# Border to the up projection: the third f pair's raw weights loaded from ScalarE's queue, and split behind the second pair's first chain

## The chip, the cores and the metric

The kernel runs on one core of one Trainium2 chip. The metric is the device time of one execution in microseconds (us), as the median of several runs. The names of the engines are those of the profile: PE is TensorE (PEld its weight loads), DVE VectorE, ACT ScalarE, POOL GpSimd, SP SyncE. SPq and ACTq are the instruction queues of SP and ACT, from which DMAs are issued.

## The reference

One inference step of a hybrid encoder layer, for 1024 prompt frames and 64 sample frames. The part that matters here is the second sub-layer, an MLP with a squared ReLU, and its first matrix product:

```python
def sq_relu_mlp(x, w_up, w_down):
    h = jnp.square(jax.nn.relu(jnp.einsum('btd,df->btf', x, w_up)))
    return jnp.einsum('btf,fd->btd', h, w_down)
...
xp = layer_norm(ALPHA * xp + mix, ln1_g[l], ln1_b[l])
xp = layer_norm(ALPHA * xp + sq_relu_mlp(xp, w_up[l], w_down[l]), ln2_g[l], ln2_b[l])
```

Here `x` has 1024 columns and `w_up` is 1024 x 4096. The layer norm ahead of it closes the mixer; the product with `w_down` follows.

## The kernel before

All matrix products run in three passes of split fp32: each operand is a high part (rounded to the PE's fp32r form by an ACT copy, line 1247 or 1531) and a low part (the difference, line 98, on POOL or DVE). The up projection goes over 16 pairs of 128 columns of `w_up` (`p`, an "f pair"), and in each pair over two groups of columns of x, `s` = 0 (288 wide, the sample frames among them) and `s` = 1 (256 wide). Each (pair, group) is one *chain* of seven products in place of eight (a Strassen-like scheme), of twelve matmuls each, at line 1309. A product needs one of seven weight operands: 0, 1 and 3 are raw quarters of the pair's weights (tile `wa`), 2, 4, 5 and 6 are sums of quarters (tile `ws`).

The seven products of a chain add into four PSUM banks named zA, zB, zC and zD:

```python
PROD = ((0, 0, "A"), (1, 1, "B"), (5, 4, "A"), (4, 3, "D"), (6, 5, "A"), (3, 6, "C"), (2, 2, "D"))
```

So products 0, 2 and 4 add into the same bank zA, and between them ACT copies the bank out (line 1320): product 2 waits for ACT's copy of product 0, product 4 for that of product 2. Products 3 and 6 share zD: product 6 waits for DVE's sum at line 1323, which reads zD and the copy of product 4. DVE also makes the sums at 1325 (zB), 1327 (zC) and 1329 (zD after product 6). `relu` (line 1341) squares, `sums` (lines 1350 to 1353) makes the h operands of the down projection, and SP stores them (`h4_dr` at line 1354, `h3_dr` at 1355, `hs_dr` at 1358).

The weights of a pair are prepared by `prep`: the raw 1 MB is loaded into tile `wr` (line 1500 before, 1501 after the change), three quarters are split into `wa` (high halves by ACT at 1247; low halves at 98 by POOL, for pair 2 the first of them by DVE), `summed` forms the sums in place in `wr` by four DVE operations (1256, 1257, 1259, 1260), `high` and `low` split these into `ws` (1531 by ACT, 98 by DVE).

The stretch around the change is the *border* between the mixer and the steady loop over the pairs. There the order of each engine's instructions is written out by hand (`with in_order(border)`: each instruction is chained behind the one before it on its engine). First the two chains of pair 0 run, then the weights of pair 1 are prepared, then its chains `ch` (s = 0) and `ch1` (s = 1), and beside them the weights of pair 2 are prepared. From pair 2 on, the order of PE is kept by hand for pair 2 and otherwise found by a planner, which puts instructions in the order in which it expects them to be ready.

The framework adds the semaphores. Each DMA reports on one of eight semaphores (DMAHW0 to DMAHW7), taken in turn; the queue that issues a DMA first waits until the DMA that used the same semaphore before has landed. In the border the two stores of h of chain (0, 1), from the tiles `y`, take semaphores 4 and 5; those of chain (0, 0), from `h`, take 6, 7, 0, 1 and 2; the two halves of pair 2's raw load take 3 and 4.

Of the kernel before, what the change touches and what calls it, by code (L numbers as in the profile page):

```python
# [49 lines left out]
def build(tc, a):  # L50
    nc = tc.nc
    es = ExitStack()
    with es:
        _build(nc, tc, a, es)


def _build(nc, tc, a, es):
    def trows(t):
        return P if t < NB else TS
# [9 lines left out]
    w_up = a["w_up"].rearrange("l d e -> (l d) e").rearrange("(k p) e -> p k e", p=P)  # L69
# [30 lines left out]
    @contextmanager  # L100
    def in_order(prev=None, only=None):

        traced = nc.cur_bb.bb.instructions
        last = traced[-1]
        yield
        at = next(k for k in reversed(range(len(traced))) if traced[k] is last) + 1
        prev = {} if prev is None else prev
        for i in traced[at:]:
            if only is not None and i.engine != only:
                continue  # L110
            p = prev.get(i.engine)
            if p is not None:
                tc.add_manual_dep(i, p.name, mybir.DependencyInfo(
                    mybir.DependencyClass.NoSync, mybir.DependencyReason.DATA), reason="in_order")
            prev[i.engine] = i
# [53 lines left out]
    def two_halves(nm, sa, tag):  # L169
        if sa is not None:  # L170
            return [sa.tile([P, 512], F32, name=f"{nm}_{i}", tag=tag, bufs=10) for i in range(2)]
        r = sp.tile([P, D], F32, name=nm, tag="row", bufs=ROWS)
        return [r[:, 0:512], r[:, 512:D]]

    def prep(t, sa):
        n = trows(t)
        o = two_halves(f"oo{t}", sa, "kp")
        if sa is not None:
            uu = sa.tile([P, 256], F32, name=f"uu{t}", tag="uu", bufs=2)
            sqs = [sa.tile([P, 512], F32, name=f"sq{t}", tag="sq", bufs=1)] * 2  # L180
        else:
            uu = sp.tile([P, 256], F32, name=f"uu{t}", tag="gl", bufs=3)
            sqs = [sp.tile([P, 512], F32, name=f"sq{t}_{i}", tag="raw", bufs=2) for i in range(2)]
        nc.sync.dma_start(uu[0:n], u_dr[t * P:t * P + n, :])
        ss = sp.tile([P, 16], F32, name=f"ss{t}", tag="ss", bufs=2)
        for i in range(2):
            oh = o[i][0:n]
            nc.sync.dma_start(oh, o_dr[t * P:t * P + n, i * 512:(i + 1) * 512])
            c = slice(384, 512) if i == 0 else slice(0, 128)
            nc.gpsimd.tensor_tensor(oh[:, c], oh[:, c], uu[0:n, i * P:(i + 1) * P], op=ALU.mult)  # L190
            sq = sqs[i]
            nc.scalar.activation(sq[0:n], oh, AF.Square)
            sh = ss[0:n, i * 8:(i + 1) * 8]
            nc.vector.tensor_reduce(sh, sq[0:n].rearrange("p (h c) -> p h c", c=DH), axis=AX.X, op=ALU.add)
            nc.vector.scalar_tensor_tensor(sh, sh, 1.0 / DH, env["rge"][0:n, t, i * 8:(i + 1) * 8],
                                           op0=ALU.mult, op1=ALU.add)
            nc.gpsimd.tensor_tensor(sh, sh, negh[0:n].broadcast_to([n, 8]), op=ALU.pow)
            o3 = oh.rearrange("p (h c) -> p h c", c=DH)
            nc.vector.tensor_tensor(o3, o3, sh.unsqueeze(2).broadcast_to([n, 8, DH]), op=ALU.mult)
        os_[t] = o  # L200
# [89 lines left out]
    with ExitStack() as p1:  # L290
# [818 lines left out]
        while f_live or a_live:  # L1109
# [11 lines left out]
            if go_a:  # L1121
# [5 lines left out]
                try:  # L1127
                    c = next(A)
# [8 lines left out]
            elif f_live:  # L1137
                try:
                    c = next(F)
# [355 lines left out]
    with p3:  # L1495
        def up_load(p):
            r = lp.tile([P, KT, 256], F32, name=f"wr{p}", tag="wr")

            for c in ((0, P), (P, 256)) if p == 2 else ((0, 256),):
                nc.sync.dma_start(r[:, :, c[0]:c[1]], w_up[:, :, p * 256 + c[0]:p * 256 + c[1]])  # L1500
            return r[:, :, 0:P], r[:, :, P:256], r

        def prep(p, rest=True, raw=None):
            raw = raw or up_load(p)
            pool = rp if p % 2 else lp
            wa = pool.tile([P, 3, 2, 4, P], F32R, name=f"wa{p}", tag="wa")
# [39 lines left out]
        def chain(p, s):  # L1546
            sn = lp.tile([P, 2 + s, NS[s]], F32, name=f"sn{p}_{s}", tag=f"sn{s}")
            h8 = lp.tile([P, 8, NS[s]], F32, name=f"hh{p}_{s}", tag=f"hh{s}")
            return Chain(p, s, sn, lambda a, b: h8[:, a:b], ((2, 6),))
# [4 lines left out]
        with in_order(border):  # L1554
# [27 lines left out]
            summed, high, low = prep(1, False, raws1)  # L1582
# [18 lines left out]
        for tag, n in (("wa", 3072), ("wr", 2048), ("hh1", 2048), ("sn1", 768), ("sn0", 768), ("hh0", 2304), ("ws", 4096),  # L1601
                       ("hx", 1024)):

            lp.tile([P, n], F32, name=f"at_{tag}", tag=tag)
        with in_order(border):
            raw = up_load(2)
            ch = chain(1, 0)
            for i in range(6):
                ch.product(i)
            ch.product(6, False)  # L1610
            ch1 = chain(1, 1)
            ch1.product(0)
            ch1.product(1)
            ch.relu()
            ch1.product(2)
            ch.sums()
            ch1.product(3)
            ch1.product(4)
            summed, high, low = prep(2, False, raw)
            summed()  # L1620
            high()
            ch1.product(5)
            low()
            ch1.product(6)
# [9 lines left out]
        ch = chain(NP - 3, 1)  # L1634
        for i in range(7):
            ch.product(i)
        ch = chain(NP - 3, 0)
        for i in range(7):
            ch.product(i, False)
        summed, high, low = prep(NP - 1, False)  # L1640
# [81 lines left out]
    with ExitStack() as p3:  # L1722
# [229 lines left out]
        for c in range(NC - 1):  # L1952
            for part in range(2):
# [8 lines left out]
                ch = [Down(g, x) for x in range(2)]  # L1962
# [31 lines left out]
        c = NC - 1  # L1994
        fixed = {b: ps.tile([P, 512], F32, name=f"last{b}", tag=tag, bufs=2) for b, tag in (("B", "s"), ("D", "pt"))}
        gbp = []
        ch = [Down(2 * c + k // 2, k % 2, fixed, norm) for k in range(4)]
# [154 lines left out]
```

## Time and profile before

| what | us |
|---|---|
| median of three runs (lowest to highest) | 1384.46 (1384.05 to 1385.76) |
| the profiled execution, its own time | 1385.9 |
| its span, from the first instruction to the last | 1384.0 |
| PE busy in the span | 1320.5 |
| DVE, ACT, POOL busy | 998.8, 719.5, 611.3 |

The profiled execution lies 1.4 us above the median, and 1.9 us of its time lie outside the span. The border to the up projection lies at about 680 to 725 us from the span's start, the steady loop over pairs 2 to 15 from there to about 1045 us, the down projection behind it. In a timeline row the columns are start, length, engine, line, operation, out<-in, count, and in brackets the engine's idle time before the row and what ended it. In rows by stretch each engine has its busy time with the number of instructions in brackets, and the last three columns are the clock granted to PE (1.00 is full speed), the busy share of the DMA engines and GB/s.

### The profile page before, as it was taken

Reading aid. Unit: us, or ns where it says so; the run is one execution under the profiler, and the core shown is the slowest. Engines: PE = TensorE matmul, PEld = TensorE weight load, DVE = VectorE, ACT = ScalarE, POOL = GpSimd, SP = SyncE. Lnnn points to the kernel's source line nnn. Section 1 sums busy time; section 2 is a strip of 40 time slices with the busy share of each in tenths; the row PEclk is TensorE's granted clock in tenths of the full one; section 3 lists DMA queues with packets and bytes.
Section 4 is the critical chain, followed back from the end, with each engine's and each line's share of the span. In section 5 each row is a group of like instructions: output and inputs, shape, how many; then the busy total and the mean of one; then the engine's idle time right before and its main releaser. Section 6 shows DMA issues by size and latency. Waiting matters only on the chain.

```text
span 1384.0 us, 24332 instructions
## 1 busy us (share of the span) xinstructions
PE 1320.5 (95%) x8827; PEld 1202.0 (87%) x8827; DVE 998.8 (72%) x1797; ACT 719.5 (52%) x1561; POOL 611.3 (44%) x666
## 2 busy tenths in 40 slices
PE   7999999999988998999999999999999999999996
PEld 7899989989887987778899999999987787887774
DVE  4577566576788288679886868778678677767677
ACT  4367556566656466334523232223267676767665
POOL 3232222255675355666412212212167675655557
PEclk9999999999999999999999999999999999999999
DMA  7445465131302247532234444354468334434343
GB/s 226 105 122 154 155 190 135 52 96 46 90 21 66 66 138 248 185 109 86 77 115 143 135 153 142 119 169 141 161 218 301 116 137 164 141 119 156 101 135 130
DMA packets 159088, 185.64 MB, mean 134 GB/s; under 512 B 27756, under 2 KB 117164, under 8 KB 158968
## 3 DMA queue, kind: packets, MB, share of 16 engines
q1 hardware_dynamic: 157912, 184.06, 42.1%
q8 instruction: 70, 1.15, 0.4%
q14 instruction: 50, 0.41, 0.1%
q10 hardware_dynamic: 1056, 0.02, 0.0%
HBM read 117.65 MB, written 60.10 MB: 128 GB/s over the span
## 4 chain that ended last, share of the span: by engine, by line
PE 66%; DVE 11%; DMA 8%; ACT 6%; POOL 4%; issue 4%; SPq 0%; ACTq 0%; DVEq 0%; POOLq 0%
PE A L1774 10%; PE zA L1309 9%; PE zD L1309 6%; PE mx L251 5%; PE D L1774 5%; PE kvsb L368 5%; PE kvfox L368 4%; PE zB L1309 3%; PE zC L1309 3%; DMA rwo<-w_out 3%; PE B L1774 2%; DVE snsb L551 1%; PE qsb L509 1%; PE qfox L509 1%; PE Ssb L567 1%
## 5 line engine op out<-in xcount | busy, mean ns | idle before, releaser
L98 POOL TENSOR_TENSOR wa<-wr,wa 128x512 fp32r<-128x512 f32 x41 | 62.0, 1540 | 224.3 <-ACT wa L1247 198.7
L98 POOL TENSOR_TENSOR wd<-rd,wd 128x512 fp32r<-128x512 f32 x77 | 101.2, 1326 | 108.6 <-ACT wd L1247 108.5
L251 PE MATMUL mx<-xT,oTb 128*128 128x512 f32 (+1 forms) x416 | 104.9, 404 | 1.4 <-DVE oTb L98 1.4
L1309 PE MATMUL zD<-xo,ws 128*128 128x288 f32 (+1 forms) x720 | 97.8, 289 | 2.6 <-DVE h4a L1473 1.5
L1309 PE MATMUL zA<-xo,ws 128*128 128x288 f32 (+1 forms) x720 | 97.0, 289 | 0.0
L1309 PEld LDWEIGHTS zD<-xo,ws 128*128 128x128 f32 x720 | 93.5, 189 | 3.3 <-DVE h4a L1473 1.7
L368 PE MATMUL kvfox<-wkvfox,xT 128*128 128x256 f32 (+3 forms) x624 | 91.3, 295 | 2.7 <-ACT wkvfox L344 2.5
L251 PEld LDWEIGHTS mx<-xT,oTb 128*128 128x128 f32 (+1 forms) x416 | 76.1, 188 | 20.1 <-DVE oTb L98 2.3
L1309 PEld LDWEIGHTS zA<-xo,ws 128*128 128x128 f32 x720 | 93.4, 189 | 0.0
L1441 POOL TENSOR_TENSOR rd<-rd 128x512 f32<-128x512 f32 x56 | 79.3, 1416 | 28.9 <-DVE b L98 26.6
L553 POOL TENSOR_TENSOR sgsb<-sgsb,snsb 128x127 f32<-128x127 f32 (+7 forms) x48 | 58.4, 1218 | 73.2 <-DVE snsb L551 66.0
L368 PE MATMUL kvsb<-wkvsb,xT 128*128 128x256 f32 (+1 forms) x624 | 88.5, 287 | 0.0
L1247 ACT ACTIVATE wd<-rd 128x512 fp32r<-128x512 f32 x105 | 63.6, 624 | 46.4 <-POOL rd L1441 23.3
L1774 PE MATMUL A<-wd,wd 128*128 128x512 f32 x312 | 83.6, 396 | 3.2 <-DVE acc L1741 2.3
L368 PEld LDWEIGHTS kvfox<-wkvfox,xT 128*128 128x128 f32 (+1 forms) x624 | 82.5, 195 | 3.7 <-ACT wkvfox L344 2.9
L551 DVE TENSOR_TENSOR_SCAN snsb<-snsb,one 128x128 f32<-128x128 f32 (+7 forms) x48 | 72.6, 1515 | 15.3 <-ACT snsb L550 14.7
L368 PEld LDWEIGHTS kvsb<-wkvsb,xT 128*128 128x128 f32 (+1 forms) x624 | 79.4, 187 | 0.2
L1320 ACT ACTIVATE sn<-zA 128x256 f32<-128x256 f32 (+1 forms) x80 | 30.9, 389 | 85.4 <-PE zA L1309 71.4
L1774 PEld LDWEIGHTS A<-wd,wd 128*128 128x128 f32 x312 | 58.1, 188 | 19.6 <-DVE acc L1741 4.0
L1774 PE MATMUL A<-wd,h4a 128*128 128x512 f32 x240 | 64.7, 395 | 0.8 <-POOL wd L98 0.3
L1531 ACT ACTIVATE ws<-wr 128x1024 fp32r<-128x1024 f32 x28 | 29.2, 1058 | 61.3 <-DVE wr L1259 61.3
L1774 PEld LDWEIGHTS A<-wd,h4a 128*128 128x128 f32 x240 | 44.7, 188 | 12.6 <-POOL wd L98 0.8
(551 smaller groups left out, 3748.1 us busy)
## 6 DMA issues: line engine op xcount, KB each, us to landing
h_dr<-hh SPq DMA_DIRECT2D x30, 512.0 KB, 3.2
rd<-w_down SPq DMA_DIRECT2D x30, 512.0 KB, 4.4
wr<-w_up SPq DMA_DIRECT2D x13, 1024.0 KB, 5.5
hr<-h_dr SPq DMA_DIRECT2D x31, 384.0 KB, 4.8
h_dr<-hh SPq DMA_DIRECT2D x30, 384.0 KB, 3.6
raw<-w_in SPq DMA_DIRECT2D x44, 256.0 KB, 3.5
wo_dr<-swo SPq DMA_DIRECT2D x32, 256.0 KB, 2.5
xT<-wo_dr SPq DMA_DIRECT2D x8, 1024.0 KB, 8.4
```

The costliest lines, as they stand in the source:

```text
L98: eng.tensor_tensor(out, src, hi.bitcast(F32), op=ALU.subtract)
L251: nc.tensor.matmul(acc[0:m], oT[:, k, hx, 0:m], wo[k // 4][hw][:, k % 4, cs], start=(i == 0), stop=(i == len(seq) - 1))
L368: nc.tensor.matmul(acc[0:n, c0:c0 + n1 - n0], xT[k // 4][:, k % 4, c:c + n], wt[:, k, hw, n0:n1], start=(i == 0), stop=(i == len(seq) - 1))
L509: nc.tensor.matmul(acc[:, 0:w], wq[:, k, hw, :], xT[k // 4][:, k % 4, c:c + w], start=(i == 0), stop=(i == len(seq) - 1))
L551: nc.vector.tensor_tensor_scan(g[:, 0:n][:, ::-1], g[:, 0:n][:, ::-1], one.broadcast_to([P, n]), 1.0, op0=ALU.mult, op1=ALU.bypass)
L553: nc.gpsimd.tensor_tensor(s[:, 0:n - 1], s[:, 0:n - 1], g[:, 1:n], op=ALU.mult)
L1247: nc.scalar.activation(hi, raw, AF.Copy)
L1309: nc.tensor.matmul(z, w[:, hw, k], xop(s, bo, hx)[:, k, :], start=(new and k == 0 and j == 0), stop=(k == 3 and j == 2), skip_group_check= ...
L1320: nc.scalar.activation(c, z, AF.Copy)
L1441: eng.tensor_tensor(r[:, o], r[:, x], r[:, y], op=ALU.subtract)
L1531: nc.scalar.activation(ws[:, 0, q, c], src[:, q], AF.Copy)
L1774: nc.tensor.matmul(z, h[:, hx, q, o], wset[self.c % 2][q][:, hw, wb], start=((n in (0, 3) or n == 1 and self.c == 0) and q == 0 and j == 0 ...
```

## The change

The raw load of pair 2 is issued from ACT's queue instead of SP's, and at another place: behind `ch`'s product 0 instead of ahead of the chain. In the program as built, its two halves stand on ACT between the copy of product 0 and that of product 2; on SP they stood behind all seven stores of h of pair 0. The three splits into `wa` move ahead of `ch1`'s products (on ACT: behind the copy of `ch`'s product 4 and ahead of all three copies of `ch1`; before, behind all three). The four sums of `summed` move ahead of `ch1`'s product 4; on DVE they now stand ahead of the sum at 1323 that `ch1`'s product 6 waits for.

```diff
             for c in ((0, P), (P, 256)) if p == 2 else ((0, 256),):
-                nc.sync.dma_start(r[:, :, c[0]:c[1]], w_up[:, :, p * 256 + c[0]:p * 256 + c[1]])
+
+                (nc.scalar if p == 2 else nc.sync).dma_start(r[:, :, c[0]:c[1]], w_up[:, :, p * 256 + c[0]:p * 256 + c[1]])
             return r[:, :, 0:P], r[:, :, P:256], r
...
         with in_order(border):
+            ch = chain(1, 0)
+            ch.product(0)
             raw = up_load(2)
-            ch = chain(1, 0)
-            for i in range(6):
+            for i in range(1, 6):
                 ch.product(i)
             ch.product(6, False)
+            summed, high, low = prep(2, False, raw)
             ch1 = chain(1, 1)
             ch1.product(0)
             ch1.product(1)
@@
             ch1.product(2)
             ch.sums()
             ch1.product(3)
+            summed()
             ch1.product(4)
-            summed, high, low = prep(2, False, raw)
-            summed()
             high()
             ch1.product(5)
             low()
```

The waits of the load's two issues, in the program as built: the first waits for DMAHW3 (the store of the layer norm's last rows, issued long before), DMAHW2 and DVE (the first low half of `ws` of pair 1); the second for DMAHW4, that is, for the landing of the store `h4_dr<-y` of chain (0, 1). Beyond the border, the planner's order differs in pairs 2 to 5 (on PE, the first 19 matmuls of pair 3 stand ahead of the last products of pair 2, not behind them); from pair 6 on every engine has the same order as before.

## The prediction

> **What bounds the kernel now.** I read the page first, then busy time by stretch around the border, then the timelines of the single engines there. By the page PE is the bound, and the border is one of the few stretches where it pauses:
>
> ```profile
> PE 1320.5 (95%) x8827; PEld 1202.0 (87%) x8827; DVE 998.8 (72%) x1797; ACT 719.5 (52%) x1561; POOL 611.3 (44%) x666
> ```
> ```profile
> 720.00:730.00 10.00, 8.42 (x67) 8.21 (x67) 9.69 (x12) 3.34 (x6) 2.96 (x2) 1.00 0.24 60
> ```
>
> Where PE pauses, its timeline says:
>
> ```profile
> 705.68 1.75 PE L1309 MATMUL zA<-xo,ws 128*128 128x288 f32 x12
> 707.27 1.75 PE L1309 MATMUL zC<-xo,wa 128*128 128x288 f32 x12
> 709.71 1.87 PE L1309 MATMUL zD<-xo,ws 128*128 128x288 f32 x12 [0.69 <-DVE hh L1323]
> 711.41 1.58 PE L1309 MATMUL zA<-xo,wa 128*128 128x256 f32 x12
> 712.83 1.58 PE L1309 MATMUL zB<-xo,wa 128*128 128x256 f32 x12
> ...
> 719.93 1.59 PE L1309 MATMUL zD<-xo,ws 128*128 128x256 f32 x12
> 721.35 0.29 PE L1309 MATMUL zA<-xo,wa 128*128 128x288 f32 x1
> 723.22 1.06 PE L1309 MATMUL zA<-xo,wa 128*128 128x288 f32 x6 [1.58 <-POOL wa L98]
> ```
>
> The first three rows are `ch`'s products 4, 5, 6; then come `ch1`'s 0, 1 and 6, then pair 2. Products start 1.59 us apart (705.68 to 707.27). Product 6 was due at 707.27 + 1.59 = 708.86 and started at 709.71: 0.85 us lost to the sum at 1323. Pair 2's second matmul was due 0.13 us (1.59 / 12) behind 721.35 and came at 723.22: 1.74 us lost to POOL's low half of `wa`. All there is to gain here is 0.85 + 1.74 = 2.59 us, 0.19% of 1384.46; 0.2%, or 2.77 us, is about what a measurement of this kernel can tell from no change.
>
> Why POOL was late, ACT's timeline shows:
>
> ```profile
> 701.12 0.41 ACT L1320 ACTIVATE sn<-zA 128x288 f32<-128x288 f32 x1
> 704.29 0.41 ACT L1320 ACTIVATE sn<-zA 128x288 f32<-128x288 f32 x1 [2.76 <-PE zA L1309]
> 707.47 0.41 ACT L1320 ACTIVATE hh<-zA 128x288 f32<-128x288 f32 x1 [2.76 <-PE zA L1309]
> ...
> 718.71 0.38 ACT L1320 ACTIVATE sn<-zA 128x256 f32<-128x256 f32 x1 [2.46 <-PE zA L1309]
> 718.99 1.14 ACT L1247 ACTIVATE wa<-wr 128x512 fp32r<-128x512 f32 x2
> ```
>
> The split at 718.99 follows ACT's last copy at once, so its place behind that copy held it. An earlier load and split do remove the 1.74 us; the question is what they put in its place.
>
> **The load on ACT's queue.** The second half's issue waits for DMAHW4, the landing of the store that SP issues at 705.03:
>
> ```profile
> 705.03 0.32 SPq L1354 DMA_DIRECT2D h_dr<-y  x1
> 705.83 0.32 SPq L1355 DMA_DIRECT2D h_dr<-y  x1
> ```
> ```profile
> h_dr<-y SPq DMA_DIRECT2D x1, 384.0 KB, 2.7
> y<-w_up SPq DMA_DIRECT2D x2, 512.0 KB, 4.5
> ```
> ```profile
> L904 ACTq DMA_DIRECT2D rawf<-w_in x2: 451/488/526, 0.8 to 1.3; - x2
> ```
> ```profile
> L1354 SPq DMA_DIRECT2D h_dr<-hh x30: 320/515/578, 717.2 to 1044.4; - x30
> ...
> DMA to landing us min/median/max: 2.6/3.2/7.0
> ```
>
> Behind the waiting issue on ACT stands the copy of `ch`'s product 2 (704.29), and product 4, due at 705.68, waits for that copy. The store's own landing isn't shown. The stores of this line took 2.6 to 7.0 us; I take the 2.7 us of its sibling, issued 0.8 us behind it: 705.03 + 2.7 = 707.73. Then the issue, 0.49 us (the middle of ACT's only two), and the copy, 0.41 us: 708.63. Product 4 starts 708.63 - 705.68 = 2.95 us late. From below the cost is 0, if the wait doesn't hold ACT; with a landing of 7.0 us it is 7.25. No row of before shows ACT waiting for a DMA ahead of an issue. POOL, though, sat 25.67 us in front of its waits, with a DMA named as the last of them:
>
> ```profile
> 720.21 2.96 POOL L98 TENSOR_TENSOR wa<-wr,wa 128x512 fp32r<-128x512 f32 x2 [25.67 <-DMA h_dr<-hh]
> ```
>
> so engines do take their waits in order, and I take the 2.95. The page "DMA: Bandwidth & Descriptors" of the Trainium skill (section "Anatomy of one DMA — SWDGE (gpsimd) path") says that DMA engines don't wait on semaphores and that the issuing sequencer does so ahead of dispatch; no run here shows it for ACT.
>
> With the copies late, the 0.85 us at product 6 go: the copy of product 4 comes 1.79 us (707.47 - 705.68) after its start, and DVE, whose older work ends as before, is free by then. Net lateness there: 2.95 - 0.85 = 2.10 us.
>
> The load itself isn't late. Issued at 707.73, it lands at 712.2 with the 4.5 us of an equal load. The three high halves take three times 0.57 us (1.14 / 2), to 713.9; `ch1`'s product 0 ends at 711.41 + 1.58 + 2.10 = 715.09, so its copy isn't held. POOL's two low halves (2.96 us) end by 717, long before pair 2. The 1.74 us go. On SP the two issues leave; nothing there is later for that.
>
> **The sums ahead of the sum at 1323.** DVE's rows of before, and the operations that now stand between:
>
> ```profile
> 714.50 0.42 DVE L1325 TENSOR_TENSOR hh<-zB,sn 128x256 f32<-128x256 f32 x1 [2.44 <-PE zB L1309]
> ...
> 717.49 0.42 DVE L1353 TENSOR_TENSOR hh<-hh 128x256 f32<-128x256 f32 x1
> 719.13 0.42 DVE L1323 TENSOR_TENSOR hh<-zD,sn 128x256 f32<-128x256 f32 x1 [1.22 <-ACT sn L1320]
> ```
> ```profile
> L1256 DVE TENSOR_TENSOR wr<-wr x14: 677/679/1673, 720.4 to 985.9; 128x512 f32<-128x512 f32 x14
> ```
>
> After product 1's end DVE works without a break from 714.50 to 717.91 (relu and the sums of `ch`). Then come the four sums of `summed`, 4 x 0.68 = 2.72, then 1323, 0.42: 721.05 on the old clock, where product 6 started at 719.93. So `ch1`'s product 6 waits 1.12 us for DVE. Both ends move with product 1, so the 2.10 us change nothing here. From below it is 0 (DVE gets ahead while PE is slow elsewhere); from above two of the four cost 1.67 each, as the longest of the row, which ran beside POOL: 1.12 + 2.0 = 3.1. POOL is through by 717 here, so I take 1.12.
>
> What follows is covered: the sums' split into `ws` is done some 2 us earlier against pair 2 than before, and in pairs 2 to 5 the planner's other order moves copies and splits by a few us, in a stretch in which PE never pauses:
>
> ```profile
> 740.00:760.00 20.00, 20.00 (x161) 20.00 (x160) 13.83 (x25) 6.99 (x12) 3.78 (x3) 1.00 0.45 148
> 760.00:780.00 20.00, 20.00 (x160) 20.00 (x159) 17.49 (x24) 6.13 (x12) 4.26 (x3) 1.00 0.44 148
> ```
>
> ACT is idle there for two thirds of the time. I cost it at 0; if that cover fails, one late copy of some 0.4 us is the size.
>
> **PE's clock.** A pause of 2.95 us has a second price. These rows are from the mixer:
>
> ```profile
> 401.05 3.74 PE L368 MATMUL sgv<-wv,xT 128*128 128x256 f32 x20 [1.86 <-DVE sgvv L767]
> ```
> ```profile
> 402.00:403.00 1.00, 1.00 (x8) 1.00 (x7) 1.00 (x2) 0.26 (x1) 0.92 (x2) 0.60 0.02 4
> 403.00:404.00 1.00, 1.00 (x7) 1.00 (x7) 0.91 (x3) 0.20 (x1) 1.00 (x2) 0.50 0.45 127
> 404.00:405.00 1.00, 1.00 (x6) 1.00 (x6) 0.97 (x2) 0.21 (x1) 1.00 (x2) 0.50 0.00 0
> 405.00:406.00 1.00, 1.00 (x9) 1.00 (x8) 1.00 (x1) 0.53 (x2) 0.84 (x1) 0.69 0.00 0
> ```
> ```profile
> 54.86 0.66 PE L567 MATMUL Sfox<-kpfox,qdfox 128*128 128x128 f32 x2 [3.11 <-DMA qdfox<-qdfox]
> ```
> ```profile
> 56.00:58.00 2.00, 2.00 (x12) 2.00 (x11) 1.97 (x2) 0.00 (x0) 0.00 (x0) 0.50 1.14 267
> ```
>
> A pause of 1.86 us in a dense stream was followed by half clock: the shortfalls 0.40, 0.50, 0.50 and 0.31 add up to 1.71 us lost. A pause of 3.11 us was followed by half clock too. The 1.58 us pause of the border was not (clock 1.00 in the row for 720 to 730). A pause of 2.95 us is nearest to the 3.11: I take one stretch of half clock, 1.71 us. It falls on `ch`'s products 4 to 6, ahead of the DVE race above, so it adds. From below 0, from above two stretches, 3.4.
>
> The page "TensorE: Matmul & The Clock Gate" of the Trainium skill (Part 1) says that the gate halves the clock after an idle window of about 3.4 us, windows running freely. By that sentence 2.95 us fill no window and the sum would be 1.71 us smaller; the drop after 1.86 us here speaks against taking it so strictly.
>
> **The sum.** +2.95 - 0.85 + 1.12 - 1.74 + 1.71 = +3.19 us. The profiled execution, 1385.9 with a span of 1384.0, would become 1389.1 and 1387.2; it was 1.4 above the median. On the median: 1384.46 + 3.19 = 1387.65.
>
> **The rivals.** *No loss of clock*: the pause falls so that the gate doesn't act, as at 721. The sum is then +1.48: 1385.9, within 0.2%. For it: only some pauses were followed by half clock. Against: 1.86 us sufficed.
>
> *ACT isn't held*: the store has landed when ACT gets there, or the wait stops nothing behind it. Then the 0.85 and the clock stay as they were, and -1.74 + 1.12 = -0.62: 1383.8, not slower. It decides from a landing before 704.3, where SP's issue at 705.03 stands against it; only if the wait isn't what I read would it go so. Were DVE's 1.12 hidden too, it would be -1.74, 1382.7; even with both old pauses gone it ends at 1381.9, not faster by 0.2%.
>
> *ACT held longer*: the store or the load lands late. A store landing of 3.2 us in place of 2.7 adds 0.5; of 7.0 adds 4.3, and with two stretches at half clock 1.7 more: +5 to +9, 1389.5 to 1393. Against: its sibling's 2.7.
>
> **How the numbers follow.** The forecast, held with one stretch at half clock, gets 0.57, in a band from +2.4 to +4.2 (store landing 2.6 to 3.2, DVE's race 0.8 to 1.6); nearly four fifths of it, 0.45, lie above 2.77. No loss of clock gets 0.18, ACT not held 0.10 (0.02 of it for a gain of over 0.2% by something that I don't see), held longer 0.12, and 0.03 I keep for the reordering in pairs 2 to 5, half and half. Slower: 0.45 + 0.12 + 0.01 = 0.58. Faster 0.02. Same: 0.40. The range leaves out the not-held case and the upper part of held-longer: from 1384.7 (below the no-clock case by its bounds) to 1390.0.
>
> **What would show it.** Right: ACT idle from about 702 to 708 with a DMA of h as the releaser; a PE pause of about 3 us ahead of a zA row at 708.6 released by ACT at 1320; a stretch at 0.50 right after; no pause at product 6 of `ch`; one of 1.1 us ahead of the last zD of `ch1`, released by DVE at 1323; none ahead of pair 2. Wrong: ACT's copy still near 704.3, or the load's landing named in front of `wa`, or new pauses of PE behind 725.

## The result, and the profile after

| what | before | after |
|---|---|---|
| median of 20 runs each (lowest to highest), us | 1384.78 (1380.77 to 1389.14) | 1388.63 (1383.51 to 1392.64) |
| the profiled execution, its own time and span, us | 1385.9, 1384.0 | 1390.92, 1389.2 |

The ratio is 1.0032 with a 95% interval of 1.0023 to 1.0041: the change makes the kernel slower by 4.4 us (3.2 to 5.7); the two medians alone lie 3.9 us apart. The forecast was +3.2 us, a median of 1387.6.

The view of busy time by stretch (columns as in the prediction) has for the border of the changed kernel:

```profile
700.00:710.00 10.00, 7.18 (x47) 6.94 (x46) 8.01 (x17) 0.79 (x3) 0.00 (x0) 0.89 0.59 189
720.00:730.00 10.00, 8.93 (x73) 8.74 (x72) 9.23 (x16) 3.19 (x5) 0.00 (x0) 1.00 0.57 172
```

In the first ten microseconds PE lost 2.8 us, ACT worked for 0.79 us only, and the mean granted clock was 0.89; in the second row one pause is left, of about 1 us. PE's timeline of the changed kernel says which products these are:

```profile
702.94 1.74 PE L1309 MATMUL zD<-xo,ws 128*128 128x288 f32 x12
707.51 2.96 PE L1309 MATMUL zA<-xo,ws 128*128 128x288 f32 x12 [2.82 <-ACT sn L1320]
710.26 2.24 PE L1309 MATMUL zC<-xo,wa 128*128 128x288 f32 x12
712.34 1.75 PE L1309 MATMUL zD<-xo,ws 128*128 128x288 f32 x12
...
721.04 1.57 PE L1309 MATMUL zC<-xo,wa 128*128 128x256 f32 x12
723.68 1.69 PE L1309 MATMUL zD<-xo,ws 128*128 128x256 f32 x12 [1.07 <-DVE hh L1323]
725.21 3.20 PE L1309 MATMUL zA<-xo,wa 128*128 128x288 f32 x24
```

Product 4 of `ch` (second row) was due at 702.94 + 1.59 = 704.53 and came at 707.51, 2.98 us late. Products 4 and 5 then took 2.75 and 2.08 us in place of 1.59. Product 6 followed without a pause; the old one is gone. Product 6 of `ch1` was due at 721.04 + 1.42 = 722.46 (products of the 256 wide group start 1.42 us apart) and came 1.22 late. Ahead of pair 2, where POOL was waited for before, nothing is left. ACT's timeline shows the hold:

```profile
699.97 0.41 ACT L1320 ACTIVATE sn<-zA 128x288 f32<-128x288 f32 x1
700.38 6.62 ACTq L1501 DMA_DIRECT2D wr<-w_up  x2
707.04 0.41 ACT L1320 ACTIVATE sn<-zA 128x288 f32<-128x288 f32 x1 [6.67 <-DVE h L1350]
710.50 0.41 ACT L1320 ACTIVATE hh<-zA 128x288 f32<-128x288 f32 x1 [3.05 <-PE zA L1309]
711.28 1.67 ACT L1247 ACTIVATE wa<-wr 128x512 fp32r<-128x512 f32 x3 [0.37 <-DMA wr<-w_up]
```

Between the copies of products 0 and 2 stand the two issues, a stretch of 6.62 us. The row of this source line (shortest, median and longest issue in ns, then the starts of the first and the last) and SP's timeline, beside the waits listed under the change, say what the second one waited for:

```profile
L1501 ACTq DMA_DIRECT2D wr<-w_up x2: 375/375/375, 700.4 to 706.6; - x2
```
```profile
703.97 0.32 SPq L1354 DMA_DIRECT2D h_dr<-y  x1
704.76 0.32 SPq L1355 DMA_DIRECT2D h_dr<-y  x1
```

An issue took 0.375 us; the first began at 700.4, the second at 706.6, that is 2.6 us after SP issued the store whose semaphore it shares. The copy of product 2 could only follow it. The bracket names DVE's 1350 as releaser, and not the store that the prediction expected to find there. That is an inference from events in time; the first experiment shows that this copy needs no such thing.

The granted clock behind the pause, in stretches of 1 us:

```profile
707.00:708.00 1.00, 0.49 (x3) 0.50 (x4) 0.96 (x4) 0.41 (x1) 0.00 (x0) 0.94 0.17 44
708.00:709.00 1.00, 1.00 (x6) 1.00 (x5) 0.22 (x1) 0.00 (x0) 0.00 (x0) 0.50 0.57 117
709.00:710.00 1.00, 1.00 (x6) 1.00 (x5) 0.00 (x0) 0.00 (x0) 0.00 (x0) 0.50 1.02 292
710.00:711.00 1.00, 1.00 (x6) 1.00 (x6) 0.06 (x1) 0.41 (x1) 0.00 (x0) 0.50 1.12 379
711.00:712.00 1.00, 1.00 (x8) 1.00 (x8) 0.40 (x1) 0.72 (x2) 0.00 (x0) 0.85 1.08 383
```

The shortfalls 0.06 + 0.50 + 0.50 + 0.50 + 0.15 add up to 1.71 us. Last, POOL's low halves and DVE's end of the four sums in the changed kernel:

```profile
712.51 2.54 POOL L98 TENSOR_TENSOR wa<-wr,wa 128x512 fp32r<-128x512 f32 x2 [19.05 <-ACT wa L1247]
```
```profile
722.60 0.69 DVE L1260 TENSOR_TENSOR wr<-wr 128x512 f32<-128x512 f32 x1
723.21 0.42 DVE L1323 TENSOR_TENSOR hh<-zD,sn 128x256 f32<-128x256 f32 x1
```

POOL begins 7.7 us earlier than before (720.21; 6.6 us earlier counted from the start of `ch`'s product 1), and 1323 follows straight on the last of the sums.

**The border's length.** Whole times scatter by several us, and an experiment has 6 to 12 of them (one in the repeats), set against runs of before taken beside them, so the kernels below are compared by the border, read from one profile each: from the start of `ch`'s product 1 (its zB row) to the zB row of pair 2. That was 700.92 to 726.21 before, 25.29 us, and is 699.77 to 728.24 after, 28.47: +3.18 us. Some expectations reckon from `ch`'s product 0 instead, which makes it 26.90 before.

### The profile page after: what moved, and what is told of

Its sections match the earlier page's. It is cut to its first block, busy times and chain, and to the rows that moved or that the text cites. A ratio compares the mean times of both kernels' runs of the same rounds, so it can differ in the third digit from the quotient of the medians.

```text
span 1389.2 us, 24331 instructions
## 1 busy us (share of the span) xinstructions
PE 1324.4 (95%) x8827; PEld 1206.1 (87%) x8827; DVE 995.7 (72%) x1797; ACT 718.6 (52%) x1561; POOL 613.9 (44%) x666
## 4 chain that ended last, share of the span: by engine, by line
PE 67%; DVE 10%; DMA 8%; ACT 6%; issue 4%; POOL 4%; SPq 1%; ACTq 0%; DVEq 0%; POOLq 0%
PE A L1776 10%; PE zA L1309 9%; PE zD L1309 6%; PE mx L251 5%; PE kvsb L368 5%; PE D L1776 5%; PE kvfox L368 4%; PE zC L1309 3%; PE zB L1309 3%; DMA rwo<-w_out 2%; PE B L1776 2%; DMA raw<-w_in 1%; DVE snsb L551 1%; PE sgv L368 1%; PE qsb L509 1%
## 5 line engine op out<-in xcount | busy, mean ns | idle before, releaser
L98 POOL TENSOR_TENSOR wa<-wr,wa 128x512 fp32r<-128x512 f32 x41 | 65.0, 1613 | 224.5 <-ACT wa L1247 224.5
```

The lines of the kernel that those rows point to most:

```text
L98: eng.tensor_tensor(out, src, hi.bitcast(F32), op=ALU.subtract)
```

## The experiments

The theory is that of the prediction: ACT is held by the second issue's wait for a store's landing, PE's clock halves after the pause, and the four sums put a new wait ahead of `ch1`'s product 6. The rivals: the load's place or size is what costs, or the loss of clock has nothing to do with the pause, or something in the planner's order in pairs 2 to 5.

**One transfer in place of two.** No second issue, so no wait for the store; the rest as in the change.

```diff
-            for c in ((0, P), (P, 256)) if p == 2 else ((0, 256),):
+            for c in ((0, 256),):
```

> The raw load of pair 2 is issued on ACT as one transfer of 1 MB, not as two halves; nothing else differs from the changed kernel (PE, DVE, POOL and SP have the same instructions in the same order). It takes one completion semaphore, DMAHW3, whose last user landed long before, so ACT has nothing to wait for. The border is measured from the start of the second pair's first product to the start of pair 2's second pair of products (first zB row): 26.90 us before, 30.09 after. Theory (the wait for the store of h holds ACT, and PE's pause of 2.8 us halves its clock): the pause in front of product 4 and the stretch at half clock go, the 0.85 us in front of product 6 come back, the 1.1 to 1.2 us in front of the last zD of the second group stay: border 26.2 to 26.5, time 0.5 us below before. Rival (a DMA issue on ACT costs ACT some 6.6 us by itself, whatever it waits for): the pause stays, border about 30.

Measured: 0.9990 of before (0.9978 to 1.0002), median 1383.53. The border is 24.82, 0.47 less than before (26.44 from product 0). ACT's and PE's timelines of this kernel:

```profile
697.67 0.38 ACTq L1501 DMA_DIRECT2D wr<-w_up  x1
700.44 0.41 ACT L1320 ACTIVATE sn<-zA 128x288 f32<-128x288 f32 x1 [2.76 <-PE zA L1309]
```
```profile
705.93 1.85 PE L1309 MATMUL zD<-xo,ws 128*128 128x288 f32 x12 [0.77 <-DVE hh L1323]
...
717.36 1.68 PE L1309 MATMUL zD<-xo,ws 128*128 128x256 f32 x12 [1.07 <-DVE hh L1323]
```

The copy waits for PE alone, so DVE's 1350 was never its releaser. The pause ahead of product 4 and the half clock are gone, the old pause at product 6 of `ch` is back, and the new one of `ch1` stays. The hold is the second issue's, not the load's.

**Three pieces.** A third issue shares its semaphore with the next store (1355), issued 0.79 us later.

```diff
-            for c in ((0, P), (P, 256)) if p == 2 else ((0, 256),):
+            for c in ((0, P), (P, 192), (192, 256)) if p == 2 else ((0, 256),):
```

> The changed kernel with the load in three pieces (the second half cut in two). The third takes semaphore DMAHW5, whose last user is the second store of h from y, issued 0.8 us behind the first and landing 0.8 to 1.0 us later. Theory (ACT is held until the store on the same semaphore has landed): the pause in front of product 4 grows from 2.98 us to 3.8 to 4.4 (0.8 to 1.0 for the store, up to 0.4 for the third issue), and the half clock costs 1.7 or, with two windows, 3.4 us: border 29.2 to 31.5 in place of 28.47. Rival (the hold is a fixed cost of the first DMA issues on ACT): the pause stays at 3.0, border 28.5.

Measured: 1.0042 (1.0026 to 1.0059), border 29.15 (+3.86). ACT's timeline and PE's row:

```profile
700.54 7.50 ACTq L1501 DMA_DIRECT2D wr<-w_up  x3
708.09 0.41 ACT L1320 ACTIVATE sn<-zA 128x288 f32<-128x288 f32 x1 [7.46 <-DVE h L1353]
```
```profile
708.55 3.25 PE L1309 MATMUL zA<-xo,ws 128*128 128x288 f32 x12 [3.61 <-ACT sn L1320]
```

The hold grew from 6.62 to 7.50 us, by 0.88, where a third issue by itself would add 0.375, and product 4 came 3.76 late in place of 2.98: the hold follows the store that is waited for. The pause of 3.6 us cost one stretch of half clock, as that of 2.8 did, and pause and border came just below the lower end of what was expected.

**PE kept busy in the pause.** 24 matmuls of no use, on operands that are ready, ahead of product 4.

```diff
+                if i == 4:
+                    fill = ps.tile([P, 512], F32, name="fill", tag="pt", bufs=2)[:, 0:256]
+                    for _ in range(24):
+                        nc.tensor.matmul(fill, wops[1][0][:, 0, 0], xop(1, 0, 0)[:, 0, :], ...)
                 ch.product(i)
```

> The changed kernel with 24 further matmuls of 128x256 on PE in front of product 4 of the second pair's first chain, into a PSUM bank that nobody reads; they add work and change no result. ACT is held as before, but PE is busy in the pause: 24 x 0.12 = 2.9 us of work in a pause of 2.98 us. Theory (1.71 us of the loss are the half clock that follows the pause): no stretch at 0.50, border 28.3 to 28.6 in place of 30.09, time about 1.5 us above before. Rival (the clock drop belongs to something else, or costs nothing because later waits take it up): border about 30.

Measured: 1.0004 (0.9990 to 1.0018), border 26.82 (28.41 from product 0), 1.65 us less than in the changed kernel. ACT, PE and the clock by stretch:

```profile
697.72 6.60 ACTq L1501 DMA_DIRECT2D wr<-w_up  x2
704.37 0.41 ACT L1320 ACTIVATE sn<-zA 128x288 f32<-128x288 f32 x1 [6.58 <-DVE h L1350]
```
```profile
701.94 3.00 PE L1614 MATMUL fill<-xo,wa 128*128 128x256 f32 x24
704.83 1.86 PE L1309 MATMUL zA<-xo,ws 128*128 128x288 f32 x12
```
```profile
700.00:710.00 10.00, 10.00 (x79) 9.90 (x79) 6.37 (x16) 2.24 (x5) 0.19 (x1) 1.00 0.81 270
```

ACT is held as long, and product 4 starts as late (2.89 us), but the clock stays at 1.00 and products 4 and 5 take their usual time. So the 1.7 us come from PE's idleness, and from nothing else that goes on in that stretch.

**The sums behind product 4.** `summed` after `ch1.product(4)`, so that 1323 is ahead of the four sums again.

```diff
-            summed()
             ch1.product(4)
+            summed()
```

> The changed kernel with the four sums of the weights behind product 4 of the second group again, so that DVE makes the sum at 1323 ahead of them. The hold of ACT and the half clock stay. Theory (the sums stand in front of the sum at 1323 and cost product 6 1.1 to 1.2 us): no pause in front of the last zD of the second group, border 28.8 to 29.0, time about 2 us above before. Rival (the pause is not DVE's order but the late load's): the pause stays and the border is about 30.

Measured: 1.0010 (0.9996 to 1.0025), border 27.04 (28.63 from product 0), 1.43 less than after. PE's timeline:

```profile
703.65 2.88 PE L1309 MATMUL zA<-xo,ws 128*128 128x288 f32 x12 [2.74 <-ACT sn L1320]
...
718.60 1.58 PE L1309 MATMUL zD<-xo,ws 128*128 128x256 f32 x12
720.02 3.18 PE L1309 MATMUL zA<-xo,wa 128*128 128x288 f32 x24
```

The hold and the half clock stay, the wait of `ch1`'s product 6 is gone, and pair 2 doesn't wait for the later sums. The border came 0.2 us below what was expected.

**Both mended.** One transfer, and the sums behind product 4.

> The changed kernel with both losses taken away: the raw load as one transfer on ACT (nothing to wait for), and the four sums of the weights behind product 4 of the second group, so that DVE makes the sum at 1323 first. Theory: only the 0.8 us in front of product 6 of the second pair's first chain are left; no pause in front of the last zD of the second group, none ahead of pair 2, no half clock: border 23.5 to 23.8 in place of 25.29, time 1.6 us (0.12%) below before, below both kernels. Rival (the late sums are then late for pair 2's third products): a new pause of up to 1 us at pair 2's zA on ws, border 24.5, time some 0.8 below before.

Measured: 0.9979 (0.9969 to 0.9989), median 1381.87 against 1383.44, 2.9 us faster than before (1.5 to 4.3): it beats both kernels (the medians lie 1.6 us apart). The border is 23.46, 1.83 less than before and just below the lower end of what was expected. PE's timeline has one pause left in it, that of `ch`'s product 6, which was there before:

```profile
710.26 1.86 PE L1309 MATMUL zD<-xo,ws 128*128 128x288 f32 x12 [0.72 <-DVE hh L1323]
...
720.48 1.58 PE L1309 MATMUL zD<-xo,ws 128*128 128x256 f32 x12
721.90 3.17 PE L1309 MATMUL zA<-xo,wa 128*128 128x288 f32 x24
```

**The load back on SP.** All other moves kept: what is the queue alone worth, once the split stands ahead of `ch1`?

```diff
-                (nc.scalar if p == 2 else nc.sync).dma_start(r[:, :, c[0]:c[1]], w_up[:, :, p * 256 + c[0]:p * 256 + c[1]])
+                nc.sync.dma_start(r[:, :, c[0]:c[1]], w_up[:, :, p * 256 + c[0]:p * 256 + c[1]])
```

> The changed kernel with the raw load back on SP's queue, where it stands behind all stores of h of pair 0; the order of all other work is that of the changed kernel (the splits into wa ahead of ACT's three copies of the second group). All borders from the start of the second pair's second product (zB) to pair 2's first zB: 25.29 us before, 28.47 changed. Theory (it is a wait in ACT's order that costs, by whichever queue the load goes): nothing holds product 4, but the load is issued some 12.7 us after the border's start and lands 5.4 later; ACT waits for it ahead of the copy of the second group's product 0, so product 2 is about 5 us late, with one or two stretches at half clock (1.7 each) behind that pause: border 31 to 34, time 5 to 8 us above before. Rival (the place of the splits is harmless, and only the DMA issues on ACT cost): border as with the single load, 24.8, time as before.

Measured: 1.0056 (1.0039 to 1.0073), border 31.33 (+6.04). SP, ACT and PE:

```profile
709.89 1.01 SPq L1501 DMA_DIRECT2D wr<-w_up  x2
```
```profile
715.89 1.67 ACT L1247 ACTIVATE wa<-wr 128x512 fp32r<-128x512 f32 x3 [10.20 <-DMA wr<-w_up]
```
```profile
717.88 2.93 PE L1309 MATMUL zA<-xo,ws 128*128 128x256 f32 x12 [5.60 <-ACT sn L1320]
```

Behind the stores the load is issued at 709.89 and splits at 715.89, and the copy of `ch1`'s product 0 stands behind that split. The early split needs the early load: without it, it is worse than no move at all. The early load without the early split was not run.

**The load behind the copy of product 4.** Two transfers on ACT, issued when the store has landed anyway.

```diff
             ch = chain(1, 0)
-            ch.product(0)
-            raw = up_load(2)
-            for i in range(1, 6):
+            for i in range(5):
                 ch.product(i)
+            raw = up_load(2)
+            ch.product(5)
             ch.product(6, False)
```

> The changed kernel with the load's two halves issued on ACT behind the copy of product 4 rather than behind that of product 0; nothing else differs. By then the store of h has landed or is about to (issued about 3 us before). Theory (it is the wait, and what stands behind it on ACT, that costs): no pause in front of product 4, no half clock, the 0.85 us in front of product 6 as before. The load lands about 13.5 us after the border's start, later beside the stores of h; the splits then hold ACT's first copy of the second group by 1 to 2 us, and the race on DVE shrinks by as much: border 26.0 to 27.5, time within 1 us of before. Rival (a DMA issue on ACT costs ACT some 6.6 us by itself): the first copy of the second group is held by 6 us more, border above 30.

A miss: the border is 27.88, or 29.47 from product 0, where 26.0 to 27.5 was expected; the time is 1.0005 of before (0.9991 to 1.0018). ACT, PE and one row of DVE:

```profile
706.62 1.01 ACTq L1501 DMA_DIRECT2D wr<-w_up  x2
713.66 1.67 ACT L1247 ACTIVATE wa<-wr 128x512 fp32r<-128x512 f32 x3 [6.72 <-DMA wr<-w_up]
```
```profile
715.65 1.68 PE L1309 MATMUL zA<-xo,ws 128*128 128x256 f32 x12 [2.15 <-ACT sn L1320]
...
723.31 1.68 PE L1309 MATMUL zD<-xo,ws 128*128 128x256 f32 x12 [1.71 <-DVE hh L1323]
```
```profile
717.41 1.40 DVE L1350 TENSOR_TENSOR hh<-hh 128x256 f32<-128x256 f32 x1
```

ACT isn't held by the issue, as expected, but the split begins 6.7 us after the second issue (at 707.0), where the changed kernel took 711.28 - 706.6 = 4.7. The load now moves beside the stores of h, and those landed later too: 7.2 and 7.4 us after their issue (1354, 1355), where they took 5.3 and 5.5 in the changed kernel. So `ch1`'s product 2 waits. That delay doesn't shorten DVE's race, as I had thought: DVE's sum at 1325 needs the same copy, and everything behind it is late too. The wait of product 6 even grew, from 1.22 to 1.88 us. One of the operations that DVE has ahead of 1323, the sum at 1350 in the row above, took 1.40 us in place of 0.42 while POOL made its low halves (714.89 to 718.53); in the second execution of this kernel it took 1.40 again, beside POOL again. This is the upper case of the prediction's DVE term, in another kernel and by another operation. That POOL is the reason is not shown by a run of its own.

**Twice the same kernel.** Is the border's length fixed, when whole times scatter so much?

> The changed kernel once more, unchanged, for one profile. Question: is the border the same length in every execution, or does it hold a part that comes by chance? Border here is from the start of the second pair's second product (zB) to pair 2's first zB row; it was 25.29 before, 28.47 in the first profile of the changed kernel. Theory (the hold on ScalarE and the race on VectorE are fixed by the program, the half clock follows a pause of 2.9 us): the pause ahead of product 4 is 2.8 to 3.1 us, that ahead of the second chain's product 6 about 1.2 us, one stretch of half clock costs 1.6 to 1.8 us, border 28.2 to 28.8. Rival (the clock's gate acts by chance on a pause of this length): either no stretch, border 26.8, or two, border about 30.2; then the border's mean would differ from the 3.18 us of the first profile.

> The kernel with the load behind the copy of product 4 once more, unchanged, for one profile: its border was 27.88 (2.59 over before), while its times lay only 0.7 us over before (interval -1.2 to 2.5). Theory (the late landing of the load beside the stores of h is fixed by the program): the copy of the second chain's product 0 waits again for the split of the late load, pauses of 2.0 to 2.4 us ahead of product 2 and 1.5 to 2.0 ahead of product 6, border 27.4 to 28.4. Rival (the landing varies from run to run): the first pause is under 1 us, and the border under 27.

Measured: the changed kernel's border is 28.36 (28.47 the first time), that of the load behind copy 4 27.90 (27.88), with the same pauses to 0.1 us. The span, though, was 1383.1 in place of 1389.2 for the changed kernel, under the 1384.0 of the profile before (an execution of before taken beside it had 1380.5). All but 0.1 of the 6.1 us lie outside the border: 2.87 ahead of it (its start at 696.90 against 699.77), the cause of which stays open, and 3.12 behind it. For the part behind, a row by stretch of the first execution, then of the second:

```profile
1000.00:1075.00 75.00, 70.10 (x365) 59.05 (x364) 54.95 (x83) 44.45 (x89) 46.15 (x36) 0.95 0.74 256
```
```profile
1000.00:1070.00 70.00, 63.73 (x337) 52.71 (x337) 54.19 (x80) 43.25 (x87) 45.57 (x36) 1.00 0.75 260
```

Around 1020 and 1065 us, at pauses of 1.0 to 1.8 us that lie in both, the first had half clock twice (its shortfall, 0.05 of 75 us, is 3.4 to 4) and the second not at all.

**The balance.** From PE's timelines, each term as what it adds to an unbroken border: a pause with the slower start behind it (about 0.1 us each), and half clock for itself.

| kernel | ahead of a zA product | half clock | `ch` 6 | `ch1` 6 | pair 2 | sum against before | border against before | whole runs against before (95%) |
|---|---|---|---|---|---|---|---|---|
| before | | | 0.96 | | 1.83 | 0 | 0 | 0 |
| after | 2.98 | 1.65 | | 1.33 | | +3.17 | +3.18 | +4.4 (3.2 to 5.7) |
| after, again | 2.87 | 1.68 | | 1.33 | | +3.09 | +3.07 | |
| one transfer | | | 1.01 | 1.32 | | -0.46 | -0.47 | -1.4 (-3.0 to 0.3) |
| PE kept busy | 3.00 | | | 1.32 | | +1.53 | +1.53 | +0.6 (-1.4 to 2.5) |
| sums behind product 4 | 2.90 | 1.66 | | | | +1.77 | +1.75 | +1.4 (-0.6 to 3.5) |
| both mended | | | 0.98 | | | -1.81 | -1.83 | -2.9 (-4.3 to -1.5) |
| three pieces | 3.76 | 1.53 | | 1.33 | | +3.83 | +3.86 | +5.8 (3.6 to 8.2) |
| load on SP | 5.75 | 1.54 | 1.01 | 0.53 | | +6.04 | +6.04 | +7.7 (5.4 to 10.1) |
| behind copy 4 | 2.41 | | 0.98 | 1.97 | | +2.57 | +2.59 | +0.7 (-1.2 to 2.5) |

Five terms account for every border to 0.03 us. They are read from the same rows as the border, so this says only that nothing is left over; what causes a term is shown by the kernels that lack it. The whole runs agree with the border within their intervals, or at their edge: that of the load behind copy 4 ends 0.1 us short of it, and for the change itself the runs say 4.4 and the border 3.2, with an interval from 3.2. So up to 2.5 us more may be lost elsewhere, which the profiles don't settle.

## Why the prediction was right

**The hold of ACT, +2.95.** Measured 2.98 and 2.87. The landing was taken as 2.7 us from the issue of the store; the second issue started 2.6 after it. Its own price was 0.375 us, not 0.49. That the sum still came to within 0.03 of the first figure is luck: the store was issued 0.56 us ahead of the time at which product 4 was due, not 0.65, and about 0.1 us went by between issue, copy and product, which the sum left out. The ground for taking the hold was weaker than it looked. POOL's 25.67 us with a store named as releaser don't show an engine in front of its waits: POOL began at 720.21, right behind ACT's second split (718.99 + 1.14 = 720.13), which makes the inputs of its operation. What shows it is ACT's hold itself. One transfer took the hold away, and a third piece lengthened it. The sentence of the page "DMA: Bandwidth & Descriptors" of the Trainium skill (section "Anatomy of one DMA — SWDGE (gpsimd) path"), that the issuing sequencer waits ahead of dispatch, is now seen at ACT: 6.62 us for two issues, with the copy behind them.

**Product 6 of `ch`, -0.85, and pair 2, -1.74.** Both went, as said, and both were worth 0.1 us more than the gap, since the product behind a pause runs slower at its start: 0.96 and 1.83. The load was early enough: its splits started at 711.28, and POOL's low halves at 712.51. Where the hold is taken away, the pause at product 6 returns, as its step had it.

**The sums, +1.12.** 1.22, with its slower start 1.33. The step that the hold changes nothing here holds: without it (one transfer) the wait is 1.22 as well. The upper bound, sums beside POOL, wasn't reached: POOL was through at 715.05, and the sums began at 720.36.

**The clock, +1.71.** The shortfall was 1.71, of which 1.65 fell on PE's work. This was the least certain term. By the page "TensorE: Matmul & The Clock Gate" of the Trainium skill (Part 1), taken strictly, a pause under 3.4 us fills no window, and the clock would have stayed. Here pauses of 2.7 and 2.8 us were followed by half clock in three profiles of three, and PE kept busy was not: the row from the mixer was the better guide. The window's length on that page agrees: 1.71 us of shortfall is half of 3.4.

**Pairs 2 to 5, 0.** The waits of PE in the changed kernel between 690 and 1060 us (total in us, number, longest) name nothing of a reordered copy or split:

```profile
PE zA L1309 <- ACT sn L1320: 2.8, 1, 2.8
PE zD L1309 <- DVE h4a L1473: 1.8, 1, 1.8
PE A L1776 <- DVE acc L1741: 1.2, 1, 1.2
PE zD L1309 <- DVE hh L1323: 1.1, 1, 1.1
```

The first and the last are the border's, the second and the third belong to the passage to the down projection, past 1000 us. The loop's length says the same, from pair 2's zB row to the end of PE's work ahead of the wait for 1473. The row of that wait, before and after:

```profile
1015.38 1.86 PE L1309 MATMUL zD<-xo,ws 128*128 128x288 f32 x12 [1.48 <-DVE h4a L1473]
```
```profile
1017.69 2.60 PE L1309 MATMUL zD<-xo,ws 128*128 128x288 f32 x12 [1.79 <-DVE h4a L1473]
```

That is 1015.38 - 1.48 - 726.21 = 287.69 us before and 1017.69 - 1.79 - 728.24 = 287.66 after; in the other nine profiles it comes to 287.66 or 287.67. So the planner's other order cost nothing in the profiled executions, and what whole runs may lose beyond the border isn't lost in the loop.

The steps that came out off, by up to 0.2 us (the sums), cancel: +3.19 forecast, +3.18 and +3.07 found. The order of events was foreseen; the agreement to 0.01 is luck. The rival "ACT isn't held" was a real case, only for another kernel: with one transfer its -0.62 came out as -0.47. The forecast on the whole time was right by a narrow edge: its own sum was 0.23%, and single executions scatter by more than that, so only the mean of many shows it.

## What to carry to other kernels

A DMA put on a compute engine's queue brings its waits with it, the wait for the semaphore's former user among them, and the engine's work behind it stood still here, for 6.6 us: look up which transfer used that semaphore last and when it lands, and don't split a load into a piece whose semaphore is still in use. A pause taken from one place is only a gain if the operations that move with it don't cross a race elsewhere; here a load in one piece and sums a product later turned +3.2 us into -1.8 us of border. Where whole times scatter by more than the change, measure the stretch that it touches, between two of the bound engine's own rows.

## What the runs showed of the hardware that was not expected

Half clock came in stretches that cost 1.7 us each, and pauses of 1 to 2 us on the passage to the down projection were followed by it in one execution and not in another of the same program; that is part of why the span of the changed kernel was 1383.1 us once and 1389.2 once, with the same border. In the border it followed after each pause of 2.7 to 3.6 us (four profiles), and not after those of 2.15 and 2.19 us in the two profiles of the load behind copy 4, though one of 1.86 us in the mixer sufficed: the length alone doesn't decide. A pause of 5.60 us was followed by two stretches in a row (the load on SP), but half of it passed while PE stood still, so that it cost 1.54 us. The first product behind a pause takes about 0.1 us more at full clock. And a releaser named in a bracket can be wrong by kind: for the held copy it was DVE, and the runs point to the landing of a store, which no view shows directly.
